# SwiGLU quads in Strassen form: the two 256-column products written as 512-column matmuls, and two of four weight sums moved to GpSimd

## The chip, the cores and the metric

The kernel runs on one core of a Trainium2 chip. The metric is the device time of one execution in microseconds (us); less is better. In the profile PE is the matmul engine (TensorE), PEld its weight load, DVE the VectorE, ACT the ScalarE, POOL the GpSimd and SP the SyncE, which here issues the loads. Tile names in the profile begin with the part of the program that they belong to: a0 and b0 are the first and the second SwiGLU block (FFN) of layer 0, a1 and b1 those of layer 1, m0 and m1 the mixers between a layer's two FFNs. They run in the order a0, m0, b0, a1, m1, b1.

## The reference

```python
SEQ = 512; D_MODEL = 1024; D_FF = 2816; DEPTH = 2

def swiglu(x, w_gu, w_down):
    g, u = jnp.split(x @ w_gu, 2, axis=-1)
    return (jax.nn.silu(g) * u) @ w_down

h = x
for i in range(DEPTH):
    h = h + 0.5 * swiglu(rmsnorm(h, ffn1_norm[i]), ffn1_w_gu[i], ffn1_w_down[i])
    ...   # mixer: convolution, attention, gates, w_o
    h = h + 0.5 * swiglu(rmsnorm(h, ffn2_norm[i]), ffn2_w_gu[i], ffn2_w_down[i])
    ...   # gated input embedding
return rmsnorm(h, final_norm)
```

Everything is fp32. The change touches the four SwiGLUs alone, and in them the product with `w_gu` (1024 x 5632) and the first steps of the product with `w_down`.

## The kernel before

**Numbers.** An fp32 operand is split into a high part h and a low part l of the type fp32r, so that one fp32 product takes three matmuls: h by h, h by l, l by h. For weights the split is ACT's copy `wh` (line 72) and DVE's difference `wl` (line 73), each on a tile of 128 x 1024 that holds eight 128 x 128 weight tiles.

**Strassen.** `w_gu` is computed in quads. A quad takes two features' gate and up columns (a11, a12, a21, a22 are the four quarter blocks of its weights, each one 128 x 1024 tile `st`) and both halves of the 512 rows (256 rows each), and replaces eight quarter products with seven, numbered by j = 1 to 7 (`step`). Class `Quad` forms the weight operands out of the quarters: a11, a12 and a22 as they are, and four sums, all on DVE: a11 - a21 (line 153), a22 - that = s (155), a21 + a22 (158) and a12 - s (150). Class `Halved` forms the operands on the side of the activations, once for each FFN.

**Two ways to issue a product.** A product has h·h, h·l and l·h parts over 4 row blocks and 2 weight tiles each. `joint` (P1, P2, P3, P4, P6) sends h and l of the activations as one operand of 512 columns (`wide`: 8 matmuls with `wh`), and then the high part alone by `wl` (`narrow`: 8 matmuls of 256 columns). The 512 columns land in the two halves of a PSUM tile (`[:, :, :H]` and `[:, :, H:]`), which are added when the tile is read: ACT copies one half, and DVE adds the other (`out`, lines 559 and 560). `product` (P5, P7) sends 24 matmuls of 256 columns, all into one half.

**Chains.** P1 fills tile b. ACT copies b into a new tile a (`seed`, line 555), and P2 adds to a. P6 adds to b, and ACT copies b into d. P5 adds to the right half of d, which ACT then copies out as c5; P7 adds to the left half of b, and DVE adds c5 (line 582), which is one output; P3 adds to d, P4 to b. The PSUM pools PB (tiles b, and whole projections) and PA (tiles a and d) each hold two such tiles.

**Order.** An FFN ends each quad's output with `finish` (a multiply by the row norm on DVE, SiLU on ACT, a multiply on DVE) and with a split of the result into h and l. `next_quad` puts the steps of two successive quads in a row: P1 of the next, P4 of this one, a fill, P2, P6, a fill, P5, P7, P3, two fills. A fill is one accumulation of the down projection: 12 matmuls of 512 columns into a tile `pd`, over four features. The first FFN (a0) does four features without quads and 9 quads; the others do two features and 10 quads each, 39 in all. A scheduler then places every engine's instructions by the dependences and its own costs, so an engine's order can differ from the program's text; each engine executes its own list in order and waits on semaphores of the others. SP loads the raw weights `st` ahead, as far as buffers come free.

Of the kernel before, what the change touches and what calls it, by code (L numbers as in the profile page):

```python
# [130 lines left out]
class Quad:  # L131


    def __init__(self, W, quarters):
        self.W = W
        for q in ("a11", "a21", "a22", "a12"):
            setattr(self, q, W.raw(quarters[q]))

    def part(self, j):

        W = self.W
        tt = W.nc.vector.tensor_tensor
        if j == 1:
            return W.split(self.a11)
        if j == 2:
            return W.split(self.a12)
        if j == 4:
            return W.split(self.a22)
        if j == 3:
            tt(self.a12, self.a12, self.s, ALU.subtract)  # L150
            return W.split(self.a12)
        if j == 6:
            tt(self.a11, self.a11, self.a21, ALU.subtract)  # L153
            self.s = W.buffer("s")
            tt(self.s, self.a22, self.a11, ALU.subtract)  # L155
            return W.split(self.s)
        if j == 5:
            tt(self.a21, self.a21, self.a22, ALU.add)  # L158
            return W.split(self.a21)
        return W.split(self.a11)  # L160

# [22 lines left out]
def trunk_kernel(ctx, tc, dims, x, p, positions, gains, rope_c, final_row, weights, out):  # L184
# [52 lines left out]
    def PB(name):  # L237
        return two(banks.chain, name)
# [211 lines left out]
    class Halved:  # L450


        def __init__(self, nm, l, name):
            self.nm, self.l, self.name = nm, l, name
            self.ys = {p_: [] for p_ in range(1, 8)}
            self.half = {}

# [9 lines left out]
        def own(self, j, xs):  # L467

            H = S // 2
            left, right = slice(0, H), slice(H, S)  # L470
            x, t = G(f"{self.name}x{j}"), G(f"{self.name}t{j}")
            nc.scalar.mul(x, h[j], gain(self.nm, self.l, j))
            nc.vector.tensor_tensor(t[:, left], x[:, right], x[:, left], ALU.subtract)
            th, tl = G(f"{self.name}t{j}h", F32R), G(f"{self.name}t{j}l", F32R)
            self.ys[1].append(self.both(xs[j], left))
            self.ys[5].append((th[:, left], tl[:, left]))
            self.half[j] = x, t, th, tl

        def other(self, j, xs):

            H = S // 2
            left, right = slice(0, H), slice(H, S)
            k = j + KD // 2
            x, t, th, tl = self.half.pop(j)
            y, u = G(f"{self.name}y{j}"), G(f"{self.name}u{j}")
            nc.scalar.mul(y, h[k], gain(self.nm, self.l, k))
            nc.vector.tensor_tensor(t[:, right], y[:, right], x[:, right], ALU.subtract)
            nc.vector.tensor_tensor(u[:, left], t[:, right], x[:, left], ALU.add)
            nc.vector.tensor_tensor(u[:, right], y[:, left], u[:, left], ALU.subtract)
            split_to(th, tl, t)  # L490
            self.ys[7].append((th[:, right], tl[:, right]))
            for p_, at in ((2, left), (3, right)):
                self.ys[p_].append(self.both(xs[k], at))
            for p_, at in ((6, left), (4, right)):
                v = G(f"{self.name}u{j}_{p_}", F32R).rearrange("p (a t) -> p a t", t=H)
                split_to(v[:, 0, :], v[:, 1, :], u[:, at])
                self.ys[p_].append((v[:, 0, :], v))

    class Sevens:
# [7 lines left out]
        def __init__(self, w, l, name, ys, columns, done):  # L507
            self.w, self.l, self.name, self.ys, self.columns, self.done = w, l, name, ys, columns, done
            self.todo = {}
            self.narrow_first = ()  # L510

        def quad(self, n):
            if n not in self.todo:
                cs = self.columns(n)
                quarters = {f"a{a_ + 1}{b_ + 1}": [(self.w, self.l, (4 * b_ + k) * P, c) for k in range(4) for c in cs[a_]]
                            for a_ in range(2) for b_ in range(2)}
                self.todo[n] = {"w": Quad(W, quarters)}
            return self.todo[n]

        def tile(self, n, what):  # L520
# [2 lines left out]
        def joint(self, ps, d, j):  # L523

            hi, lo = d["w"].part(j)
            at = [slice(i * P, (i + 1) * P) for i in range(8)]
            def wide(last):
                for k, (_, pair) in enumerate(self.ys[j]):
                    for w in range(2):
                        nc.tensor.matmul(ps[:, w, :].rearrange("p (a t) -> p a t", t=self.H), hi[:, at[2 * k + w]], pair,  # L530
                                         start=j == 1 and k == 0, stop=last and k == 3, skip_group_check=True)

            def narrow(last):
                for k, (vh, _) in enumerate(self.ys[j]):
                    for w in range(2):
                        nc.tensor.matmul(ps[:, w, :self.H], lo[:, at[2 * k + w]], vh, start=False, stop=last and k == 3,
                                         skip_group_check=True)

            parts = (narrow, wide) if j in self.narrow_first else (wide, narrow)
            for i, part in enumerate(parts):  # L540
                part(i == 1)
# [12 lines left out]
            d[what] = PA(f"{self.name}{n}{what}")  # L554
            nc.scalar.copy(d[what].rearrange("p w t -> p (w t)"), d["b"].rearrange("p w t -> p (w t)"))

        def out(self, n, ps, f, c):
            t = self.tile(n, f"o{f}{c}")
            nc.scalar.copy(t, ps[:, :, self.H:])
            nc.vector.tensor_tensor(t, ps[:, :, :self.H], t, ALU.add)  # L560
            self.done(n, f, c, t, t)

        def step(self, n, j):
# [8 lines left out]
            elif j == 6:  # L572
                self.joint(d["b"], d, j)
                self.seed(n, "d")
            elif j == 5:
                self.product(d["d"][:, :, H:], d, j)
                d["c5"] = self.tile(n, "c5")
# [13 lines left out]
    def ffn(l, nm, name, first=False, beside=iter(()), early=2):  # L591
# [2 lines left out]
        nf = DFF // P  # L594
        W.close()
        acts = {}
        ys = Halved(nm, l, name)
        n_whole = 4 if first else 2
        n0 = n_whole // 2

# [1 line left out]
        def finish(n, f, c, src, t):  # L602
# [9 lines left out]
            if whole:  # L612
# [41 lines left out]
        def fill():  # L654
            if downs:
                m, f0 = downs.pop(0)
                down(m, f0, f0 + 4)

        def next_quad(n):

            for i, j in enumerate((1, 4, None, 2, 6, None, 5, 7, 3, None, None)):
                next(beside, None)
                if j is None:
                    if i < 9 or downs and downs[0][1] < f_last:
                        fill()
                    continue
                step(n if j == 4 else n + 1, j)
                if j == 6 and n % 2:
                    downs.extend((m, 2 * n - 2) for m in range(KD))
# [43 lines left out]
        else:  # L713
# [624 lines left out]
```

## Time and profile before

| what | value |
|---|---|
| median of three runs | 2251.29 us (2251.19 to 2251.89) |
| profiled execution | 2251.37 us, of which the span of instructions is 2249.2 us |
| granted TensorE clock, mean | 0.999 |
| PE busy | 2240.2 us, 100% of the span, 12140 matmuls |
| DVE busy | 1743.6 us, 78% |
| ACT busy | 1455.7 us, 65% |
| POOL busy | 37.3 us, 2%, 42 instructions |
| loads (queue q1) | 220.28 MB, 29.2% of the DMA engines' time |

A row of the timeline has the start in us from the span's start, the duration in us, the engine, the line of the kernel, the operation, output and inputs by name, and in brackets how long the engine was idle before it and what released it. Matmuls are pipelined: the duration of one reaches into the next, and what counts is the distance from start to start.

### The profile page before, as it was taken

The numbers are of one execution on the slowest core, as the hardware profiler recorded it, in microseconds if no ns is written. First come the engines' busy times: TensorE is split into PE (matmuls) and PEld (weight loads), VectorE is DVE, ScalarE is ACT, GpSimd is POOL, SyncE is SP. The second block draws the span as 40 slices with busy tenths as digits, with TensorE's granted clock in tenths as the row PEclk, the third lists the DMA queues.
The fourth block names the chain that finished last, engine by engine and source line by source line (L and its number), as shares of the span: only waits on it lengthen the run. The fifth ranks groups of instructions, "written<-read, shape, count | busy, mean of one in ns | idle before, by whom it ended". The sixth has DMA issues, their size and how long they took to land.

```text
span 2249.2 us, 31135 instructions
## 1 busy us (share of the span) xinstructions
PE 2240.2 (100%) x12140; PEld 1946.9 (87%) x12140; DVE 1743.6 (78%) x2454; ACT 1455.7 (65%) x2246; POOL 37.3 (2%) x42
## 2 busy tenths in 40 slices
PE   9999999999999999999999999999999999999998
PEld 8888888888888888888888888888888888888887
DVE  8987768798866887776797777687889678777756
ACT  7666666576744666667676666664767457666665
POOL 0000000000200000000000000000001000000000
PEclk9999999999999999999999999999999999999999
DMA  5333332323132232334223233323222223333331
GB/s 216 99 113 104 103 123 75 112 75 104 48 104 84 94 103 97 108 105 141 75 94 104 95 106 109 113 87 102 92 77 75 94 75 101 106 103 103 106 101 38
DMA packets 63362, 223.04 MB, mean 99 GB/s; under 512 B 7280, under 2 KB 7280, under 8 KB 63216
## 3 DMA queue, kind: packets, MB, share of 16 engines
q1 hardware_dynamic: 62640, 220.28, 29.2%
q8 instruction: 95, 1.56, 0.3%
q10 hardware_dynamic: 576, 0.79, 0.1%
q14 instruction: 51, 0.42, 0.1%
HBM read 218.94 MB, written 2.10 MB: 98 GB/s over the span
## 4 chain that ended last, share of the span: by engine, by line
PE 96%; DVE 3%; ACT 1%; issue 0%
PE b1pd L269 2%; PE a1pd L269 2%; PE b0pd L269 2%; PE a0pd L269 2%; PE b0pd L271 2%; PE a1pd L271 2%; PE b0pd L270 2%; PE b1pd L271 2%; PE b1pd L270 2%; PE a1pd L270 2%; PE a0pd L270 2%; PE a0pd L271 2%; DVE wl L73 1%; PE e1pg L1134 1%; PE e1pg L1136 1%; PE e1pg L1135 1%
## 5 line engine op out<-in xcount | busy, mean ns | idle before, releaser
L73 DVE TENSOR_TENSOR wl<-st,wh 128x1024 fp32r<-128x1024 f32 (+1 forms) x508 | 614.5, 1212 | 227.2 <-ACT wh L72 223.8
L72 ACT CAST wh<-st 128x1024 fp32r<-128x1024 f32 (+1 forms) x507 | 527.6, 1043 | 305.3 <-PE m1Bp L270 13.9
L72 ACT CAST wh<-s 128x1024 fp32r<-128x1024 f32 x49 | 51.4, 1050 | 29.2 <-PE m1Cp L270 4.2
L73 DVE TENSOR_TENSOR wl<-s,wh 128x1024 fp32r<-128x1024 f32 x49 | 59.6, 1217 | 0.3 <-ACT wh L72 0.3
L153 DVE TENSOR_TENSOR st<-st,st 128x1024 f32<-128x1024 f32 x49 | 59.7, 1218 | 0.2
L155 DVE TENSOR_TENSOR s<-st,st 128x1024 f32<-128x1024 f32 x49 | 59.7, 1218 | 0.1
L150 DVE TENSOR_TENSOR st<-st,s 128x1024 f32<-128x1024 f32 x49 | 59.6, 1216 | 0.0
L158 DVE TENSOR_TENSOR st<-st,st 128x1024 f32<-128x1024 f32 x49 | 59.6, 1216 | 0.0
L647 ACT ACTIVATE h<-a0pd 128x512 f32<-128x512 f32 x40 | 23.7, 592 | 5.6 <-PE a0pd L271 5.4
L647 ACT ACTIVATE h<-b1pd 128x512 f32<-128x512 f32 x40 | 23.6, 590 | 4.9 <-PE b1pd L271 4.8
L647 ACT ACTIVATE h<-b0pd 128x512 f32<-128x512 f32 x40 | 23.6, 590 | 4.8 <-PE b0pd L271 4.7
L647 ACT ACTIVATE h<-a1pd 128x512 f32<-128x512 f32 x40 | 23.5, 589 | 4.5 <-PE a1pd L271 4.4
L643 ACT ACTIVATE b0pd<-h 128x512 f32<-128x512 f32 x40 | 24.0, 599 | 0.6
L643 ACT ACTIVATE b1pd<-h 128x512 f32<-128x512 f32 x40 | 24.0, 599 | 0.6
L643 ACT ACTIVATE a1pd<-h 128x512 f32<-128x512 f32 x40 | 23.9, 598 | 0.7
L643 ACT ACTIVATE a0pd<-h 128x512 f32<-128x512 f32 x40 | 23.9, 599 | 0.6
L108 POOL MEMSET wh<- 128x256 f32 x4 | 1.1, 313 | 1172.8 <-DVE wl L73 1172.8
L269 PE MATMUL a0p<-a0x,wh 128*128 128x512 f32 x44 | 17.1, 390 | 0.0
L270 PE MATMUL a0p<-a0x,wh 128*128 128x512 f32 x44 | 17.1, 390 | 0.0
L271 PE MATMUL a0p<-a0x,wl 128*128 128x512 f32 x44 | 17.1, 389 | 0.0
L264 ACT ACTIVATE b1x<-h,cols 128x512 fp32r<-128x512 f32 x8 | 5.8, 724 | 13.3 <-DVE h L1063 13.3
L264 ACT ACTIVATE b0x<-h,cols 128x512 fp32r<-128x512 f32 x8 | 5.8, 724 | 13.3 <-DVE h L1063 13.3
(6949 smaller groups left out, 7502.7 us busy)
## 6 DMA issues: line engine op xcount, KB each, us to landing
st<-in_weights SPq DMA_DIRECT2D x406, 512.0 KB, 3.3
st<-in_weights SPq DMA_DIRECT2D x8, 256.0 KB, 5.2
h<-in_x SPq DMA_DIRECT2D x7, 256.0 KB, 5.3
out<-e1d SPq DMA_DIRECT2D x4, 256.0 KB, 2.1
out<-fh SPq DMA_DIRECT2D x3, 256.0 KB, 2.0
e0pi<-in_p SPq DMA_DIRECT2D x2, 256.0 KB, 4.0
e1pi<-in_p SPq DMA_DIRECT2D x2, 256.0 KB, 3.7
fg<-in_final_row SPq DMA_DIRECT2D x2, 256.0 KB, 5.0
```

What stands on the lines that cost most here:

```text
L72: self.nc.scalar.copy(hi[:, w], src[:, w])
L73: self.nc.vector.tensor_tensor(lo[:, w], src[:, w], hi[:, w].bitcast(F32), ALU.subtract)
L150: tt(self.a12, self.a12, self.s, ALU.subtract)
L153: tt(self.a11, self.a11, self.a21, ALU.subtract)
L155: tt(self.s, self.a22, self.a11, ALU.subtract)
L158: tt(self.a21, self.a21, self.a22, ALU.add)
L269: nc.tensor.matmul(ps, wh, vh, start=first, stop=False, skip_group_check=seeded)
L270: nc.tensor.matmul(ps, wh, vl, start=False, stop=False, skip_group_check=seeded)
L271: return nc.tensor.matmul(ps, wl, vh, start=False, stop=last, skip_group_check=seeded)
L643: nc.scalar.mul(ps, h[m], 2.0)
L647: nc.scalar.mul(h[m], ps, 0.5)
L1134: nc.tensor.matmul(o, vh[:, toks(t)], wh, start=first, stop=False)
```

## The change

- P5 and P7 of the FFNs become `joint` products with a 512-column operand (`fresh = (1, 7)`, `merged=True`; `Halved.other` now lays th and tl out as that operand, by two splits of 256 columns in place of one of 512). P7 gets a PSUM tile e of its own from PB and starts it afresh. c5 and P7's value are each formed by a copy and an add (`sum`), DVE adds P7's value to b, and POOL adds it to c5, which is then the output.
- Of the four weight sums a11 - a21 and a21 + a22 go to POOL, asked for at j = 1. The first goes to a buffer d of its own, and s is written over a11.
- One of the two fills at the end of `next_quad` moves between P5 and P7.
- In the FFNs other than the first, the down projections m = 0 and 1 are begun with feature 0 alone after the first quad's P3; the later fill then does the features left.

```diff
 class Quad:
@@ part
         if j == 1:
+            if self.by_pool:
+                self.d = W.buffer("d")
+                W.nc.gpsimd.tensor_tensor(self.d, self.a11, self.a21, ALU.subtract)
+                W.nc.gpsimd.tensor_tensor(self.a21, self.a21, self.a22, ALU.add)
             return W.split(self.a11)
...
         if j == 6:
-            tt(self.a11, self.a11, self.a21, ALU.subtract)
-            self.s = W.buffer("s")
+            if self.by_pool:
+                self.s, self.a11 = self.a11, self.d
+            else:
+                tt(self.a11, self.a11, self.a21, ALU.subtract)
+                self.s = W.buffer("s")
             tt(self.s, self.a22, self.a11, ALU.subtract)
             return W.split(self.s)
         if j == 5:
-            tt(self.a21, self.a21, self.a22, ALU.add)
+            if not self.by_pool:
+                tt(self.a21, self.a21, self.a22, ALU.add)
             return W.split(self.a21)
@@ Halved.other
-            split_to(th, tl, t)
-            self.ys[7].append((th[:, right], tl[:, right]))
+            if self.merged:
+                for p_, at, v in ((5, left, th), (7, right, tl)):
+                    v = v.rearrange("p (a t) -> p a t", t=H)
+                    split_to(v[:, 0, :], v[:, 1, :], t[:, at])
+                    self.ys[p_].append((v[:, 0, :], v))
+            else:
+                split_to(th, tl, t)
+                self.ys[7].append((th[:, right], tl[:, right]))
@@ Sevens
-                                         start=j == 1 and k == 0, stop=last and k == 3, skip_group_check=True)
+                                         start=j in self.fresh and k == 0, stop=last and k == 3, skip_group_check=True)
...
-        def out(self, n, ps, f, c):
-            t = self.tile(n, f"o{f}{c}")
+        def sum(self, n, what, ps):
+            t = self.tile(n, what)
             nc.scalar.copy(t, ps[:, :, self.H:])
             nc.vector.tensor_tensor(t, ps[:, :, :self.H], t, ALU.add)
+            return t
+
+        def out(self, n, ps, f, c):
+            t = self.sum(n, f"o{f}{c}", ps)
             self.done(n, f, c, t, t)
@@ Sevens.step
+            elif j == 5 and 7 in self.fresh:
+                self.joint(d["d"], d, j)
+                d["c5"] = self.sum(n, "c5", d["d"])
+            elif j == 7 and 7 in self.fresh:
+                e = PB(f"{self.name}{n}e")
+                self.joint(e, d, j)
+                p = self.sum(n, "p7", e)
+                nc.vector.tensor_tensor(d["b"][:, :, H:], d["b"][:, :, H:], p, ALU.add)
+                t = d.pop("c5")
+                nc.gpsimd.tensor_tensor(t, t, p, ALU.add)
+                self.done(n, 1, 1, t, t)
@@ ffn
+        sevens.fresh = (1, 7)
...
                 m, f0 = downs.pop(0)
-                down(m, f0, f0 + 4)
+                begun = pds.pop(m, None)
+                down(m, f0 + (begun is not None), f0 + 4, begun, first_=begun is None)
...
-            for i, j in enumerate((1, 4, None, 2, 6, None, 5, 7, 3, None, None)):
+            for i, j in enumerate((1, 4, None, 2, 6, None, 5, None, 7, 3, None)):
...
             step(n0, 7)
             step(n0, 3)
+            for m in range(2):
+                pds[m] = down(m, 0, 1, last=False)
```

How the rows move is shown at three places; "waits" lists the engines and queues whose semaphores a row waits for, and a number behind a name is a buffer's.

First the matmuls of quad 6 of the first FFN on PE. Before, from the last three matmuls of P5 (operand t0 to t3, into d) to the first three of P7 (into b):

```order
L550 MATMUL a06d<-a0t3h,wh_1825 128x256
L550 MATMUL a06d<-a0t3l,wh_1825 128x256
L550 MATMUL a06d<-a0t3h,wl_1826 128x256
L550 MATMUL a06b<-a0t0h,wh_1855 128x256
L550 MATMUL a06b<-a0t0l,wh_1855 128x256
L550 MATMUL a06b<-a0t0h,wl_1856 128x256
```

After the change, from the last matmuls of the fill that now stands between P5 and P7, over all of P7 (into e), to the start of P3:

```order
L278 MATMUL a0pd_1_1816<-a0a11l,wh_1776 128x512
L279 MATMUL a0pd_1_1816<-a0a11h,wl_1777 128x512
L545 MATMUL a06e<-a0t0l,wh_1832 128x512 x2
L545 MATMUL a06e<-a0t1l,wh_1832 128x512 x2
L545 MATMUL a06e<-a0t2l,wh_1832 128x512 x2
L545 MATMUL a06e<-a0t3l,wh_1832 128x512 x2
L551 MATMUL a06e<-a0t0l,wl_1833 128x256 x2
L551 MATMUL a06e<-a0t1l,wl_1833 128x256 x2
L551 MATMUL a06e<-a0t2l,wl_1833 128x256 x2
L551 MATMUL a06e<-a0t3l,wl_1833 128x256 x2
L551 MATMUL a06d<-a0x_161,wl_1863 128x256 x2
```

P5 is written like P7 now, and stands before the fill. The rows of 256 columns with the high and the low part of an operand have become rows of 512 columns (x2: for the two weight tiles), the tile e is new, and b is no longer touched here.

Next DVE, and POOL beside it, in the same quad. Before, DVE from the add of P7's value (line 582) over two multiplies of `finish` (606) to the third and the fourth weight split and the first weight sum (153) of quad 7:

```order
L582 TENSOR_TENSOR a06c_1853<-a06b,a06c_1853 128x512 [waits PE_49,Activation_49]
L606 TENSOR_TENSOR a06c_1853<-a06c_1853,a0r 128x512 [waits DVE_49]
L73 TENSOR_TENSOR wl_1965<-st_1955,wh_1964 128x1024 [waits DMAHW5_49,Activation_49]
L611 TENSOR_TENSOR a0an_1886<-a06c_1853 128x256 [waits Activation_49]
L153 TENSOR_TENSOR st_1955<-st_1955,st_1957 128x1024 [waits DMAHW6_49,DVE_49]
L560 TENSOR_TENSOR a06o_1909<-a06d,a06o_1909 128x512 [waits Activation_49]
L73 TENSOR_TENSOR wl_1987<-st_1679,wh_1986 128x1024 [waits Activation_49]
L606 TENSOR_TENSOR a06o_1909<-a06o_1909,a0r 128x512 [waits DVE_49]
L73 TENSOR_TENSOR wl_2032<-st_1961,wh_2031 128x1024 [waits DMAHW0_49,PE_49,Activation_49]
```

After, from c5's sum (line 575) on; 162 is the sum s, 154 the sum a12 - s, 601 the add of P7's value to b, 636 the multiply of `finish`:

```order
L575 TENSOR_TENSOR a06c_1813<-a06d,a06c_1813 128x512 [waits Activation_49]
L73 TENSOR_TENSOR wl_1926<-st_1913,wh_1925 128x1024 [waits DMAHW5_49,PE_49,Activation_49]
L162 TENSOR_TENSOR st_1913<-st_1917,d 128x1024 [waits DMAHW7_49,DVE_49,Pool_49]
L73 TENSOR_TENSOR wl_1948<-st_1647,wh_1947 128x1024 [waits PE_49,Activation_49]
L575 TENSOR_TENSOR a06p_1852<-a06e,a06p_1852 128x512 [waits Activation_49]
L601 TENSOR_TENSOR a06b<-a06b,a06p_1852 128x2x256 [waits DVE_49]
L636 TENSOR_TENSOR a06c_1813<-a06c_1813,a0r 128x512 [waits Pool_49]
L73 TENSOR_TENSOR wl_1993<-st_1919,wh_1992 128x1024 [waits DMAHW0_49,Activation_49]
L641 TENSOR_TENSOR a0an_1859<-a06c_1813 128x256 [waits Activation_49]
L154 TENSOR_TENSOR st_1919<-st_1919,st_1913 128x1024 [waits DVE_49]
```

And POOL's whole list from quad 5's last instruction to quad 8's weight sums (the st of the first pair, 1913 to 1917, are quad 7's):

```order
L603 TENSOR_TENSOR a05c_1543<-a05c_1543,a05p_1582 128x512 [waits DVE_49]
L146 TENSOR_TENSOR d<-st_1913,st_1915 128x1024 [waits DMAHW5_49,DMAHW6_49,DMAHW3_49,DVE_49]
L147 TENSOR_TENSOR st_1915<-st_1915,st_1917 128x1024 [waits DMAHW7_49,Pool_49]
L603 TENSOR_TENSOR a06c_1813<-a06c_1813,a06p_1852 128x512 [waits DVE_49]
L146 TENSOR_TENSOR d<-st_2183,st_2185 128x1024 [waits DMAHW3_49,DMAHW4_49,DMAHW1_49,DVE_49]
L147 TENSOR_TENSOR st_2185<-st_2185,st_2187 128x1024 [waits DMAHW5_49,Pool_49]
```

POOL's two sums of quad 7 (lines 146 and 147) have left DVE, which waits for the first of them at line 162; c5 goes through POOL (603), for which DVE waits at the multiply 636, and the weight split that followed that multiply's counterpart still stands behind it.

Last ACT at the first quad of b0, whose output c5 is ready before b02a is seeded. Before (578 is the copy of c5, 643 begins a down projection, 607 is SiLU, 559 a copy of `out`, 555 the seed):

```order
L578 COPY b01c_7206<-b01d 128x512 [waits PE_49,Activation_49]
L634 ACTIVATE b0gn_7208<-b0gn_7208 128x512 [waits DVE_49]
L72 CAST wh_7343<-st_7288 128x1024 [waits DMAHW3_49,PE_49]
L643 ACTIVATE b0pd_0_7395<-h_89 128x512
L261 CAST b0a1h<-b0un_7209 128x512 [waits DVE_49]
L607 ACTIVATE b01c_7206<-b01c_7206 128x256 [waits DVE_49]
L643 ACTIVATE b0pd_1_7511<-h_90 128x512
L72 CAST wh_7373<-s 128x1024 [waits PE_49]
L559 COPY b01o_7272<-b01d 128x512
L72 CAST wh_7399<-st_7397 128x1024 [waits DMAHW4_49,PE_49,Activation_49]
L555 COPY b02a<-b02b 128x1024 [waits DVE_49,PE_49]
L607 ACTIVATE b01o_7272<-b01o_7272 128x256 [waits DVE_49]
```

After (574 is the copy in `sum`, 665 and 637 SiLU, 674 begins a down projection, 570 is the seed):

```order
L574 COPY b01c_7124<-b01d 128x512 [waits PE_49,Activation_49]
L665 ACTIVATE b0gn_7127<-b0gn_7127 128x512 [waits DVE_49]
L674 ACTIVATE b0pd_0_7198<-h_89 128x512
L72 CAST wh_7248<-st_6962 128x1024 [waits DMAHW4_49,PE_49]
L674 ACTIVATE b0pd_1_7209<-h_90 128x512 [waits DVE_49]
L269 CAST b0a1h<-b0un_7128 128x512 [waits DVE_49]
L574 COPY b01p_7158<-b01e 128x512 [waits PE_49]
L72 CAST wh_7278<-st_7220 128x1024 [waits DMAHW4_49,PE_49]
L637 ACTIVATE b01c_7124<-b01c_7124 128x256 [waits DVE_49]
L72 CAST wh_7306<-st_7214 128x1024 [waits PE_49,Activation_49]
L574 COPY b01o_7188<-b01d 128x512
L570 COPY b02a<-b02b 128x1024 [waits DVE_49,PE_49]
```

The seed of b02a stands behind the SiLU of c5 in both, but c5 now comes after P7's copy, DVE's two adds and POOL's add, and both down projections are begun ahead of P7's copy.

More of the change, by code (lines that the diff above doesn't have):

```diff
@@ L131, with __init__ @@
 class Quad:
-    def __init__(self, W, quarters):
-        self.W = W
+    def __init__(self, W, quarters, by_pool=False):
+        self.W, self.by_pool = W, by_pool
         for q in ("a11", "a21", "a22", "a12"):
@@ L450, in trunk_kernel, with __init__ @@
     class Halved:
-        def __init__(self, nm, l, name):
-            self.nm, self.l, self.name = nm, l, name
+        def __init__(self, nm, l, name, merged=False):
+            self.nm, self.l, self.name, self.merged = nm, l, name, merged
             self.ys = {p_: [] for p_ in range(1, 8)}
@@ L475, in own @@
             self.ys[1].append(self.both(xs[j], left))
-            self.ys[5].append((th[:, left], tl[:, left]))
+            if not self.merged:
+                self.ys[5].append((th[:, left], tl[:, left]))
             self.half[j] = x, t, th, tl
@@ L509, in __init__ @@
             self.todo = {}
-            self.narrow_first = ()
+            self.narrow_first, self.fresh = (), (1,)
         def quad(self, n):
@@ L516, in quad @@
                             for a_ in range(2) for b_ in range(2)}
-                self.todo[n] = {"w": Quad(W, quarters)}
+                self.todo[n] = {"w": Quad(W, quarters, 7 in self.fresh)}
             return self.todo[n]
@@ L596, in ffn @@
         acts = {}
-        ys = Halved(nm, l, name)
+        ys = Halved(nm, l, name, True)
         n_whole = 4 if first else 2
@@ L656, in fill @@
                 m, f0 = downs.pop(0)
-                down(m, f0, f0 + 4)
+                begun = pds.pop(m, None)
+                down(m, f0 + (begun is not None), f0 + 4, begun, first_=begun is None)
         def next_quad(n):
-            for i, j in enumerate((1, 4, None, 2, 6, None, 5, 7, 3, None, None)):
+            for i, j in enumerate((1, 4, None, 2, 6, None, 5, None, 7, 3, None)):
                 next(beside, None)
                 if j is None:
-                    if i < 9 or downs and downs[0][1] < f_last:
+                    if i in (2, 5) or downs and downs[0][1] < f_last:
                         fill()
```

## The prediction

> **What bounds the kernel now.** I read the page first (its busy shares and the chain that ended last), then PE's waits, then PE's timeline over one quad, then the other engines' over the same stretch.
>
> ```profile
> span 2249.2 us, 31135 instructions
> ...
> PE 2240.2 (100%) x12140; PEld 1946.9 (87%) x12140; DVE 1743.6 (78%) x2454; ACT 1455.7 (65%) x2246; POOL 37.3 (2%) x42
> ...
> PE 96%; DVE 3%; ACT 1%; issue 0%
> ```
>
> ```profile
> PE idle L379 <- DVE hpi L306: 1.0, 1, 1.0
> PE m1cop L271 <- DVE wl L73: 0.3, 1, 0.3
> PE m0cop L271 <- DVE wl L73: 0.3, 1, 0.3
> PE a0pd L269 <- ACT a0a2h L261: 0.2, 1, 0.2
> ```
>
> PE is the bound: busy all through, 96% of the chain, and its waits come to 1.8 us. No wait is left to remove. The time falls only by what PE spends less, and rises by every wait that is new. The profiled execution took 2251.37 us (2.2 outside the span), 0.08 above the median of 2251.29; I forecast from 2251.4.
>
> **What PE spends.** PE's timeline of quad 6, and the first quad of b0, where no 512-column matmul comes before P1:
>
> ```profile
> 178.08 1.12 PE L536 MATMUL a06b<-a0u,wl 128*128 128x256 f32 x8
> 179.04 2.00 PE L530 MATMUL a06b<-a0u,wh 128*128 128x512 f32 x8
> 180.88 0.39 PE L269 MATMUL a0pd<-a0a8h,wh 128*128 128x512 f32 x1
> 181.11 0.39 PE L270 MATMUL a0pd<-a0a8l,wh 128*128 128x512 f32 x1
> ...
> 183.60 0.28 PE L550 MATMUL a06d<-a0t0h,wh 128*128 128x256 f32 x1
> 183.72 0.28 PE L550 MATMUL a06d<-a0t0l,wh 128*128 128x256 f32 x1
> ...
> 186.48 0.28 PE L550 MATMUL a06b<-a0t0h,wh 128*128 128x256 f32 x1
> ...
> 189.36 1.12 PE L536 MATMUL a06d<-a0x,wl 128*128 128x256 f32 x8
> ```
>
> ```profile
> 764.96 1.12 PE L536 MATMUL b01d<-b0x,wl 128*128 128x256 f32 x8
> 765.91 2.00 PE L530 MATMUL b01d<-b0x,wh 128*128 128x512 f32 x8
> 767.75 1.98 PE L530 MATMUL b02b<-b0x,wh 128*128 128x512 f32 x8
> 769.57 1.11 PE L536 MATMUL b02b<-b0x,wl 128*128 128x256 f32 x8
> 770.52 1.12 PE L536 MATMUL b01b<-b0u,wl 128*128 128x256 f32 x8
> ...
> 773.32 1.98 PE L530 MATMUL b02a<-b0x,wh 128*128 128x512 f32 x8
> ```
>
> P5 runs from 183.60 to 186.48 and P7 to 189.36, 2.88 us each, 0.12 for each of 24 matmuls. A joint product with the wide part first (P1: 767.75 to 770.52) takes 2.77: eight of 512 columns at 0.227 and eight of 256 at 0.12. The columns are the same; what goes is the fixed part of eight matmuls. So P5 and P7 save 2 x (2.88 - 2.77) = 0.22. Where 512 columns follow 256 there is a small loss: the wide part takes 765.91 to 767.75 = 1.84 behind a narrow one and 1.82 first. The fill that now follows P5's narrow part adds one such switch, about 0.03. Net 0.19 a quad. The clock was 0.999 throughout, so no gain or loss is put there. **39 quads x 0.19 = 7.4 us.**
>
> **DVE and POOL in a steady quad.**
>
> ```profile
> 180.00:210.50 30.50, 30.50 (x177) 27.04 (x176) 22.99 (x28) 19.97 (x29) 0.00 (x0) 1.00 0.32 107
> 110.00:120.00 10.00, 10.00 (x60) 8.90 (x60) 10.00 (x14) 6.53 (x10) 0.00 (x0) 1.00 0.28 91
> ```
>
> ```profile
> 183.38 1.23 DVE L73 TENSOR_TENSOR wl<-st,wh 128x1024 fp32r<-128x1024 f32 x1 [0.51 <-ACT wh L72]
> 187.63 1.23 DVE L73 TENSOR_TENSOR wl<-st,wh 128x1024 fp32r<-128x1024 f32 x1 [3.03 <-ACT wh L72]
> 189.62 0.69 DVE L582 TENSOR_TENSOR a06c<-a06b,a06c 128x512 f32<-128x512 f32 x1 [0.77 <-PE a06b L550]
> ...
> 192.43 1.21 DVE L153 TENSOR_TENSOR st<-st,st 128x1024 f32<-128x1024 f32 x1
> ...
> 220.19 0.69 DVE L582 TENSOR_TENSOR a07c<-a07b,a07c 128x512 f32<-128x512 f32 x1 [0.77 <-PE a07b L550]
> ```
>
> In one period (line 582 comes again after 30.57) DVE is busy 22.99 of 30.50 (fourth column of the first row; ACT 19.97). The change takes away two sums of 1.21 and line 582 (0.69), and adds three operations of 512 columns (c5's sum, P7's sum, the add to b): 3 x 0.69 - 2 x 1.21 - 0.69 = -1.0. ACT gets one copy more of some 0.6. The two 256-column splits in place of one in `Halved` are four times an FFN, under 0.3 us, beside PE. The change loads the same weights; SP waits for other DVE splits to free buffers, but PE's waits show none on a load. The moved fill costs PE nothing more, nor do the one-feature downs, whose matmuls the later fill lacks.
>
> What POOL costs, the trace of before shows only for other instructions, with one input from SBUF:
>
> ```profile
> 586.49 0.60 POOL L984 TENSOR_SCALAR m0s11e<-m0s11e,m0s11sm 128x128 f32<-128x128 f32 x1 [1.65 <-DVE m0s11sm L983]
> ...
> 587.82 1.20 DVE L73 TENSOR_TENSOR wl<-st,wh 128x1024 fp32r<-128x1024 f32 x1
> ...
> 587.99 3.26 POOL L984 TENSOR_SCALAR m0s11e<-m0s11e,m0s11sm 128x384 f32<-128x384 f32 x1 [0.90 <-DVE m0s11sm L983]
> ...
> 589.02 1.20 DVE L73 TENSOR_TENSOR wl<-st,wh 128x1024 fp32r<-128x1024 f32 x1
> ```
> ```profile
> L984 POOL TENSOR_SCALAR m0s20e<-m0s20e,m0s20sm 128x384 f32<-128x384 f32 x1 | 1.2, 1247 | 2.0 <-DVE m0s20sm L983 2.0
> ```
>
> From 128 to 384 columns POOL goes from 0.60 to 1.25, 2.5 ns a column; carried on, 1024 columns are 2.85 us and 512 are 1.57 (estimates from these rows). 2 x 2.85 + 1.57 = 7.3 a quad of 30.4: POOL keeps up. But beside two DVE subtractions the 384 columns took 3.26, 2.0 more, while those subtractions took their usual 1.20. So the two engines do get in each other's way, here at POOL's expense. A DVE subtraction that begins during a POOL operation isn't in this trace; it may be delayed by nothing or by the whole POOL operation.
>
> [...]
>
> I take no loss for PE in a steady quad. POOL's sums begin after the split ahead of line 162 in order, in the stretch that leads up to 187.63, where DVE idles most (the 3.03). The price of a full block there is 5.7 us, of which idle time of 3.03, 0.77 and 0.51 takes 4.3; the remaining 1.4 comes off the lead of the splits ahead of PE. The split of 183.38 is done at 184.61 and wanted by P3 at 189.36 (above): 4.75, so more than that. DVE's multiply 636 waits for POOL's line 603, 1.57 after P7's sum; the add 601 (0.69) lies beside it, so DVE stands about 0.9 a quad, which the -1.0 pays. Queued behind it are a weight split and c5's SiLU.
>
> ```profile
> 135.08 1.21 DVE L73 TENSOR_TENSOR wl<-st,wh 128x1024 fp32r<-128x1024 f32 x1
> ```
> ```profile
> 139.23 1.12 PE L536 MATMUL a04b<-a0u,wl 128*128 128x256 f32 x8
> ```
>
> This is the split with the shortest lead that I found between 60 and 150 us: ready at 136.29, used at 139.23, so 2.94 ahead. It follows a stretch in the first FFN in which DVE, with the rotary tables besides, is busy 10.00 of 10.00 (the second window above). There POOL is held off by back-to-back subtractions, line 162 comes late, and nothing idle absorbs it. Two or three quads of up to 2.85 + 0.9 each, less 1.0, add up to 5 to 8 against a lead of 2.94. Bounds: a gain of 0.2 (the wait before a0pd above may go, two sums being gone from DVE) and a loss of 5. I take a loss of 0.7, nearer the low end, since DVE only waits here for what POOL still lacks.
>
> **The starts of b0, a1, b1.** There no fill covers the first quad's end.
>
> ```profile
> 770.24 0.68 DVE L560 TENSOR_TENSOR b01o<-b01d,b01o 128x512 f32<-128x512 f32 x1
> ```
> ```profile
> 766.64 0.60 ACT L261 CAST b0a1h<-b0un 128x512 fp32r<-128x512 f32 x1
> ...
> 771.01 1.00 ACT L555 COPY b02a<-b02b 128x1024 f32<-128x1024 f32 x1
> ```
>
> Before, b01d is read out by DVE at 770.24, its PSUM is free at 770.92, the seed of b02a is done at 772.01, and P2 wants it at 773.32: 1.3 to spare. After: P3 ends at 767.75 - 0.2 = 767.5. P7's copy (0.6) follows the cast that ended at 767.24, and its sum (0.7) is done by about 768.5, so e is free before the two one-feature downs (2 x 3 x 0.227 = 1.36) end at 768.9; this wait costs nothing, with 0.4 to spare. P1 and P4 end at 774.5, and another feature (0.68), which the order has ahead of P2, at 775.2. But the seed now follows P7's sum, POOL's 1.57, the multiply 636 (0.69), a split, an L641 and a sum (1.2, 0.4, 1.2) and then b01o's sum: 768.5 + 1.6 + 0.7 + 2.8 + 0.7 = 774.3, the seed's 1.0 makes 775.3, and a delay of 0.5 by POOL 775.8. P2 waits 0.1 to 0.6, and the seed of d comes as late after it. Bounds: nothing, or 1.1 if both come late. I take 0.5, **3 x 0.5 = 1.5 us.** In the first FFN fills cover its start.
>
> **The sum:** 2251.4 - 7.4 + 0.7 + 1.5 = 2246.2 us, 0.23% less. About 0.2%, 4.5 us, is what a measurement here can tell from no change; the bound for faster is 2246.8.
>
> **Rivals.**
> - *Nothing new waits.* 2251.4 - 7.4 = 2244.0, and 2243.6 with the small wait of a0pd gone. For it: 22 of 30.4 us of DVE, and the lead of 4.75. Against: the chain above. Chance 0.2.
> - *The saving is spent in the starts and in the saturated stretch.* 3 x 1.1 and 5: 2251.4 - 7.4 + 8.3 = 2252.3 at most; half of it 2248.2. Chance 0.2.
> - [...] If DVE is blocked for every POOL operation and the 1.4 of above comes on top of a late line 162 (2.85) and the 0.9 of line 636, 5.2 in one quad passes the lead of 4.75. It decides at 7.4 / 39 = 0.19 us a quad; 0.5 a quad gives 2251.4 - 7.4 + 19.5 = 2263.5. Against it: 1.2 to 1.4 us of DVE are free behind even that in each period, so no backlog builds. [...] Chance 0.11.
> - *The 512-column rows gain nothing*, if P5 and P7 keep 2.88: 2251.4 + 2.2 = 2253.6 with my waits, 2251.4 without. Every joint product on the page speaks against it. Chance 0.03.
>
> My forecast has the rest, 0.46; its own range is 2244.8 to 2248, some two thirds below 2246.8. Faster: 0.2 + 0.31 = 0.51. Same (2246.8 to 2255.8): 0.15 + 0.19 + 0.02 = 0.36. Slower 0.13. The range from 2243.5 to 2252.3 leaves out most of the third rival and a little of the others.
>
> **What would show it.** PE's instructions fall by 39 x 16 = 624; the period of L575 on a c5 tile from quad to quad is 30.38 where L582's was 30.57. PE's waits list b02a, a12a, b12a on ACT's seed with 0.1 to 1.1 each, and a0-tiles with 0.7 in all. POOL's 1024-column rows last 2.2 to 3.3 us in idle stretches of DVE and more beside subtractions. DVE shows idle time before line 636 put down to POOL. I am wrong if PE lists waits for `wl` in the quads, if the 1024-column rows on POOL take over 5 us, or if DVE's subtractions beside POOL last or wait clearly more than 1.2 us.

## The result and the profile after

The change made the kernel slower: 2328.43 us (median of 4 runs, 2327.11 to 2330.82) against 2251.24, a ratio of 1.0344 with an interval of 1.0331 to 1.0356. I had forecast 2246.2 and a range up to 2252.3; the third rival came true in its cause, that POOL's operations block DVE, at four times its price and by another path.

One correction first. The description of the kernel before says that pool PA holds two tiles; it holds one. The tiles a and d of a quad take turns in it, so that the seed of d waits until DVE has read a out. Much hangs on this.

The page of after, the parts that answer to those of before (span, busy time, chain):

```profile
span 2325.3 us, 30316 instructions
...
PE 2252.2 (97%) x11516; PEld 1913.4 (82%) x11516; DVE 1864.2 (80%) x2470; ACT 1475.7 (63%) x2301; POOL 329.1 (14%) x159
...
PE 71%; DVE 14%; issue 8%; ACT 5%; POOL 2%; DMA 1%; ACTq 0%; POOLq 0%; DVEq 0%
```

PE has 624 matmuls fewer, as the diff says, but is no longer the whole chain. Its waits, from the longest (columns: what waits, for what, us in total, times, longest):

```profile
PE a0pd L277 <- ACT a0a7h L269: 4.5, 1, 4.5
PE a0pd L277 <- ACT a0a2h L269: 3.3, 1, 3.3
PE a13d L545 <- ACT a13d L570: 2.7, 1, 2.7
...
PE a06d L545 <- ACT a06d L570: 1.6, 1, 1.6
PE a08d L545 <- ACT a08d L570: 1.6, 1, 1.6
```

P5 of every quad in the steady row waits 1.6 us for the seed of its tile d (line 570). Quad 6 again, the same stretch as before, on DVE, on ACT (the seed) and on POOL:

```profile
192.34 1.22 DVE L73 TENSOR_TENSOR wl<-st,wh 128x1024 fp32r<-128x1024 f32 x1
193.47 0.42 DVE L641 TENSOR_TENSOR a0an<-a05o 128x256 f32<-128x256 f32 x1
194.02 3.22 DVE L73 TENSOR_TENSOR wl<-st,wh 128x1024 fp32r<-128x1024 f32 x1
197.17 2.88 DVE L270 TENSOR_TENSOR a0a11l<-a0an,a0a11h 128x512 fp32r<-128x512 f32 x1
199.97 1.21 DVE L73 TENSOR_TENSOR wl<-d,wh 128x1024 fp32r<-128x1024 f32 x1
201.11 0.68 DVE L575 TENSOR_TENSOR a06o<-a06a,a06o 128x512 f32<-128x512 f32 x1
```
```profile
201.87 1.00 ACT L570 COPY a06d<-a06b 128x1024 f32<-128x1024 f32 x1 [4.94 <-DVE a06o L575]
```
```profile
193.64 2.52 POOL L146 TENSOR_TENSOR d<-st,st 128x1024 f32<-128x1024 f32 x1 [10.60 <-DVE wl L73]
196.24 3.26 POOL L147 TENSOR_TENSOR st<-st,st 128x1024 f32<-128x1024 f32 x1
```

POOL's first sum ends at 196.16, and the split that DVE began at 194.02 ends at 197.24, 1.08 later: it did its work only when POOL was done, and lasted 3.22 in place of 1.23. The second sum ends at 199.50, and the 0.68 us of line 270 that began at 197.17 end at 200.05. POOL was held in its turn: 196.16 - 193.89 (end of line 641) and 199.50 - 197.24 are both 2.27 us, close to the 2.40 us of such a sum's shortest row. So here each holds the other out for a whole instruction. DVE loses 2.0 + 2.2 = 4.2 us, the sum that reads tile a (line 575) ends at 201.79, the seed at 202.87, and P5, due at 201.2, starts at 202.92. (A row at a0's start, shown at the end, does not fit this. These 2.27 to 2.40 us are less than the 2.85 that I had worked out for such a sum from the rows of another operation; no row of before gave the 2.2 that I named as its shortest time.)

Before, the same stretch had this margin:

```profile
179.98 0.68 DVE L560 TENSOR_TENSOR a06o<-a06a,a06o 128x512 f32<-128x512 f32 x1
```
```profile
181.08 1.00 ACT L555 COPY a06d<-a06b 128x1024 f32<-128x1024 f32 x1 [1.79 <-PE a06b L530]
```

The seed waited for P6 alone, was done at 182.08, and P5 came at 183.60: 1.5 to spare, and another 0.4 for DVE's sum. A delay of 4.2 goes through 1.9 of margin and the 0.64 that DVE idled before its last split, and 1.7 remains, in each quad.

**Where the 77 us are.** The distance from P1 to P1 of successive quads, from PE's timelines (us; "first three" is the sum of an FFN's first three distances, a0 and b0 shown; a1 and b1 are as b0, within 2.8):

| kernel | steady quad | first three, a0 | first three, b0 | time |
|---|---|---|---|---|
| before | 30.57 | 98.0 | 86.4 | 2251.2 |
| the change | 32.25 | 112.6 | 92.9 | 2328.4 |
| sums on DVE | 30.37 | 99.3 | 88.2 | 2253.9 |
| POOL sums alone, old products | 32.40 | 113.5 | 92.1 | 2328.5 |
| memsets on POOL | 30.37 | 99.2 | 87.1 | 2249.7 |
| sums held back | 30.37 | 105.8 | 90.9 | 2272.4 |
| sums in quarters | 30.37 | 107.6 | 90.4 | 2270.6 |
| one block | 30.37 | 102.9 | 88.2 | 2257.7 |
| first two quads old | 30.37 | 99.2 | 86.1 | 2247.0 |

There are 23 steady distances: 23 x 1.68 = 39 us. The twelve first ones add 14.6 + 6.5 + 9.3 + 6.5 = 37.

### The profile page after: what moved, and what is told of

Same layout as the page of the kernel before. It is cut to its first block, busy times and chain, and to the rows that moved or that the text cites. A ratio compares the mean times of both kernels' runs of the same rounds, so it can differ in the third digit from the quotient of the medians.

```text
span 2325.3 us, 30316 instructions
## 1 busy us (share of the span) xinstructions
PE 2252.2 (97%) x11516; PEld 1913.4 (82%) x11516; DVE 1864.2 (80%) x2470; ACT 1475.7 (63%) x2301; POOL 329.1 (14%) x159
## 4 chain that ended last, share of the span: by engine, by line
PE 71%; DVE 14%; issue 8%; ACT 5%; POOL 2%; DMA 1%; ACTq 0%; POOLq 0%; DVEq 0%
DVE wl L73 5%; ACT wh L72 2%; PE b1pd L278 1%; PE b1pd L277 1%; PE b1pd L279 1%; PE a0pd L277 1%; PE b0pd L277 1%; PE b0pd L278 1%; PE a0pd L278 1%; PE a0pd L279 1%; PE b0pd L279 1%; PE a1pd L277 1%; PE a1pd L278 1%; PE a1pd L279 1%; POOL d L146 1%
## 5 line engine op out<-in xcount | busy, mean ns | idle before, releaser
L73 DVE TENSOR_TENSOR wl<-st,wh 128x1024 fp32r<-128x1024 f32 (+1 forms) x508 | 673.7, 1328 | 187.4 <-ACT wh L72 174.2
L146 POOL TENSOR_TENSOR d<-st,st 128x1024 f32<-128x1024 f32 x39 | 108.4, 2778 | 664.4 <-DVE wl L73 637.1
L147 POOL TENSOR_TENSOR st<-st,st 128x1024 f32<-128x1024 f32 x39 | 122.8, 3149 | 3.1
L73 DVE TENSOR_TENSOR wl<-d,wh 128x1024 fp32r<-128x1024 f32 x39 | 50.0, 1281 | 2.5 <-ACT wh L72 2.5
L162 DVE TENSOR_TENSOR st<-st,d 128x1024 f32<-128x1024 f32 x39 | 47.7, 1224 | 2.6
L154 DVE TENSOR_TENSOR st<-st,st 128x1024 f32<-128x1024 f32 x39 | 47.5, 1219 | 0.0
L72 ACT CAST wh<-d 128x1024 fp32r<-128x1024 f32 x39 | 40.6, 1040 | 3.5 <-PE b02a L545 0.9
L72 ACT CAST wh<-s 128x1024 fp32r<-128x1024 f32 x10 | 10.5, 1052 | 12.9 <-PE m1Cp L278 4.2
```

Source lines behind the costliest of these rows:

```text
L72: self.nc.scalar.copy(hi[:, w], src[:, w])
L73: self.nc.vector.tensor_tensor(lo[:, w], src[:, w], hi[:, w].bitcast(F32), ALU.subtract)
L146: W.nc.gpsimd.tensor_tensor(self.d, self.a11, self.a21, ALU.subtract)
L147: W.nc.gpsimd.tensor_tensor(self.a21, self.a21, self.a22, ALU.add)
```

## The experiments

**All sums on DVE.**

```diff
-                self.todo[n] = {"w": Quad(W, quarters, 7 in self.fresh)}
+                self.todo[n] = {"w": Quad(W, quarters)}
```

> The change with all four weight sums of a quad on DVE again; P5 and P7 as 512-column products, the tile e, the add of c5 on POOL and the one-feature starts stay. Theory 1 (POOL's two weight sums hold up DVE's operations with two SBUF inputs, so that DVE reads tile a late, the seed of d is late and P5 waits 1.73 us): the wait of P5 on the seed is gone, the quads come every 30.4 us, and the time is 2244 to 2250 us. Theory 2 (the new chain with e, c5 and three more DVE operations is what is late, wherever the sums are formed): P5 still waits 1 us or more, DVE has 2.4 us more to do, and the time is above 2310 us.

2253.94 us, ratio to before 1.0011 (1.0002 to 1.0021). No steady quad waits, and the distance is 30.37, where 30.38 was forecast. So theory 2 falls, and the matmuls gain what was worked out. Yet the time is 4 to 10 us above theory 1's: the starts of b0, a1 and b1 lose 1.9 each, a0's 1.3, 7.0 in sum, more than the 23 x 0.20 = 4.6 that the steady quads gain.

```profile
PE b02d L545 <- ACT b02d L570: 1.5, 1, 1.5
PE a12d L545 <- ACT a12d L570: 1.5, 1, 1.5
PE b12d L545 <- ACT b12d L570: 1.5, 1, 1.5
PE a0pd L277 <- ACT a0pd L674: 1.3, 1, 1.3
```

**The sums on POOL, nothing else.** The kernel before with the `by_pool` branches of `Quad` for the FFNs' quads.

> The kernel before with only the two weight sums of each FFN quad moved to POOL; P5 and P7 as they were. Theory 1: d's buffer comes free at the same split of a fill, so POOL starts at the same place, DVE is held for about 4 us there, and P5 waits for the seed of d by 1 to 2 us in each steady quad: 2290 to 2330 us, with P5's wait on the page. Theory 2: no such wait; DVE has 2.4 us less to do, 2249 to 2255 us.

2328.54 us, 1.0342 (1.0325 to 1.0359), as theory 1 said: P5 waits 1.6 us, the distance is 32.40, and the two sums alone cost as much as the whole change. DVE's rows are those of the change:

```profile
194.89 3.22 DVE L73 TENSOR_TENSOR wl<-st,wh 128x1024 fp32r<-128x1024 f32 x1
198.03 2.88 DVE L270 TENSOR_TENSOR a0a11l<-a0an,a0a11h 128x512 fp32r<-128x512 f32 x1
```

**The add of c5 on DVE.**

```diff
-                nc.gpsimd.tensor_tensor(t, t, p, ALU.add)
+                nc.vector.tensor_tensor(t, t, p, ALU.add)
```

> The change with the add of P7's value to c5 (line 603) on DVE in place of POOL; the two weight sums stay on POOL. Theory 1: the sums still hold DVE, P5 still waits 1.7 us, 2322 to 2332 us. Theory 3 (DVE's wait for POOL's add, 0.7 us in each quad at the multiply 636, pushes the rest late): P5's wait shrinks by 0.5 us or more, below 2310 us.

2342.06 us in one run, slower than both theories said; P5 still waits 1.6, the distance settles at 32.24 again, and the starts and one or two quads behind them grow (b0's first three to 95.8). Theory 3 falls: DVE's wait for this one POOL add isn't what holds P5. About half of the 13.6 us more can be read from the granted clock: it was 0.50 for seven stretches of 3.41 us, 23.9 us in all against 10.2 in the change (0.994 in the mean against 0.997), which is 6.8 us of work. Why the starts wait longer I did not follow up.

**Memsets on POOL.**

```diff
+N_SET = 2
...
-                W.nc.gpsimd.tensor_tensor(self.d, self.a11, self.a21, ALU.subtract)
-                W.nc.gpsimd.tensor_tensor(self.a21, self.a21, self.a22, ALU.add)
+                for q in (self.d, self.a21):
+                    for _ in range(N_SET):
+                        W.nc.gpsimd.memset(q, 0.0)
```

> The change with POOL's two weight sums replaced by four memsets of 128 x 1024 on the same two buffers (so the weight sums are left out: P5, P6, P7 and P3 get other weights). POOL then only writes to SBUF, for about as long (4 x 1.1 us, from the 313 ns of a 256-column memset). Theory 1, with the block on the read side: DVE's subtractions keep 1.2 us, P5 waits for nothing, 2244 to 2252 us. Theory 1 with a block by any access of POOL to SBUF: the same stretched rows of 3 us on DVE and P5's wait of 1.5 us or more, 2315 to 2330 us.

2249.74 us in one run, the distance 30.37, as the theory of a block on the read side said. The kernel leaves both sums out. POOL wrote in the same stretch and DVE's split beside it took its usual time:

```profile
207.93 1.97 POOL L149 MEMSET d<- 128x1024 f32 x2 [10.57 <-DVE wl L74]
```
```profile
208.28 1.23 DVE L74 TENSOR_TENSOR wl<-st,wh 128x1024 fp32r<-128x1024 f32 x1
209.42 0.69 DVE L272 TENSOR_TENSOR a0a13l<-a0an,a0a13h 128x512 fp32r<-128x512 f32 x1
```

So it isn't POOL's being busy, nor its writes to SBUF; what is left is POOL's reading, an inference that no run tests alone. The other pair of memsets (193.10 to 195.07) ran earlier, beside line 164 and a split, which took their usual 1.23 and 1.22. A memset was shorter than a sum (0.95 us, not 2.4), so this shows the absence of a hold and is not a test at equal length.

**The sums held back.** POOL reads one column of quad n's first output, and the sums of quad n+1 queue behind it.

```diff
+            if f == c == 0:
+                mark = nc.gpsimd.tensor_tensor(tick, acts[i][:, 0:1], acts[i][:, 0:1], ALU.add)
+                sevens.later = lambda: tc.issue_after(mark.ins)
...
+                with self.later():
                     W.nc.gpsimd.tensor_tensor(self.d, self.a11, self.a21, ALU.subtract)
                     W.nc.gpsimd.tensor_tensor(self.a21, self.a21, self.a22, ALU.add)
```

> The change with POOL's two weight sums of quad n+1 held back until DVE has finished the first output of quad n (one 128 x 1 add on POOL reads that output, and the sums are queued behind it); the same sums on POOL, about 10 us later. Theory 1 (POOL holds DVE wherever it runs, but what cost the time is that it did so ahead of the sum that frees tile a for the seed of d): DVE's rows are still stretched to 2 to 3 us beside POOL, but P5's wait in the steady quads falls under 0.3 us and the period to 30.4; with the starts somewhat late, 2250 to 2262 us. Rival (the DVE time that POOL takes, 4 us a quad, is too much in any place): the period stays at 31.5 us or more, the time above 2295 us.

2272.38 us, 1.0094 (1.008 to 1.0107); above theory 1's range, far below the rival's. In the steady quad DVE is held for just as long, two splits taking 6.54 in place of 2.4:

```profile
193.26 2.40 POOL L147 TENSOR_TENSOR d<-st,st 128x1024 f32<-128x1024 f32 x1
195.74 3.26 POOL L148 TENSOR_TENSOR st<-st,st 128x1024 f32<-128x1024 f32 x1
```
```profile
190.46 0.68 DVE L578 TENSOR_TENSOR a06o<-a06a,a06o 128x512 f32<-128x512 f32 x1
...
193.54 6.54 DVE L73 TENSOR_TENSOR wl<-st,wh 128x1024 fp32r<-128x1024 f32 x2 [0.52 <-ACT wh L72]
```

But tile a's sum (here line 578) is already past, the hold falls where DVE idled 2.85 us with all sums on DVE, and the distance is 30.37. The same hold costs 1.7 us or nothing, by where it falls. At the starts, where DVE has no such place, the first three distances of the four FFNs grow by 23.5 us in sum.

**One sum on POOL**, the other on DVE.

```diff
-                W.nc.gpsimd.tensor_tensor(self.a21, self.a21, self.a22, ALU.add)
...
-            if not self.by_pool:
-                tt(self.a21, self.a21, self.a22, ALU.add)
+            tt(self.a21, self.a21, self.a22, ALU.add)
```

> The change with only a11 - a21 on POOL; a21 + a22 is on DVE again. Theory 1: one block of some 2 us in place of two; of the 4.2 us that DVE's sum of tile a came late, 1.73 showed on PE, so with 2 us less the wait of P5 in the steady quad is gone, period 30.4, and the time 2252 to 2262 us. Rival (it isn't the length of the block but that POOL is used there at all, since line 162 and the sums wait for it): P5 still waits 1 us or more, above 2290 us.

2303.88 us in one run; P5 still waits 1.5, as the rival had it. The rows tell why, and not for the rival's reason:

```profile
183.86 3.27 DVE L73 TENSOR_TENSOR wl<-st,wh 128x1024 fp32r<-128x1024 f32 x1
187.06 0.68 DVE L268 TENSOR_TENSOR a0a11l<-a0an,a0a11h 128x512 fp32r<-128x512 f32 x1
187.66 1.21 DVE L164 TENSOR_TENSOR st<-st,st 128x1024 f32<-128x1024 f32 x1
188.80 1.22 DVE L73 TENSOR_TENSOR wl<-d,wh 128x1024 fp32r<-128x1024 f32 x1
189.93 0.68 DVE L573 TENSOR_TENSOR a06o<-a06a,a06o 128x512 f32<-128x512 f32 x1
```
```profile
191.37 0.42 ACT L635 ACTIVATE a06o<-a06o 128x256 f32<-128x256 f32 x1 [1.75 <-DVE a06o L634]
191.70 1.01 ACT L568 COPY a06d<-a06b 128x1024 f32<-128x1024 f32 x1
```

Line 270's counterpart is no longer held, but the scheduler put the other sum (164) into the same gap, and on ACT the SiLU of that output ahead of the seed, 1.1 later than DVE freed the tile. The experiment changed two things more than the one it meant to. Leaving the second sum out altogether keeps both orders:

> The change with POOL's second sum (a21 + a22) left out altogether, so P5 has other weights; a11 - a21 stays on POOL. Unlike the version that formed the second sum on DVE, DVE's and ACT's orders around the seed of d are those of the change, so that only the number of blocks differs. Theory 1 (each POOL sum holds DVE once for about 2 us; the second of them is what makes the seed late): tile a's sum comes 2.2 us earlier than in the change, the seed of d is done 0.5 us before P5 wants it, period 30.37, and the time 2250 to 2260 us. Rival (any POOL sum in this place costs the wait): period 31.5 or more, above 2285 us.

2257.66 us in one run, distance 30.37, no wait of a steady P5, as theory 1 said:

```profile
181.53 3.28 DVE L73 TENSOR_TENSOR wl<-st,wh 128x1024 fp32r<-128x1024 f32 x1
184.74 0.68 DVE L269 TENSOR_TENSOR a0a11l<-a0an,a0a11h 128x512 fp32r<-128x512 f32 x1
...
186.48 0.68 DVE L574 TENSOR_TENSOR a06o<-a06a,a06o 128x512 f32<-128x512 f32 x1
```
```profile
187.24 1.00 ACT L569 COPY a06d<-a06b 128x1024 f32<-128x1024 f32 x1 [2.79 <-DVE a06o L574]
```

One hold of 2.0 fits into the margin; the second is what the steady quads paid for.

**Each sum in four pieces.**

```diff
-                W.nc.gpsimd.tensor_tensor(self.d, self.a11, self.a21, ALU.subtract)
-                W.nc.gpsimd.tensor_tensor(self.a21, self.a21, self.a22, ALU.add)
+                for out, x, y, op in ((self.d, self.a11, self.a21, ALU.subtract), (self.a21, self.a21, self.a22, ALU.add)):
+                    for w in (slice(c, c + 256) for c in range(0, 1024, 256)):
+                        W.nc.gpsimd.tensor_tensor(out[:, w], x[:, w], y[:, w], op)
```

> The change with each of POOL's two weight sums written as four of 256 columns. Theory 1 with a lock for each whole instruction: DVE gets in behind a POOL instruction of some 0.7 us, so that its subtraction is held once for at most 0.7 us and not 2.0, and POOL is then held by DVE; P5's wait falls from 1.73 to under 0.6 us, and the time below 2285 us. [...]

2270.62 us in one run, distance 30.37, no steady wait. DVE's splits beside POOL take 1.57 and 1.76:

```profile
186.67 5.37 POOL L148 TENSOR_TENSOR d<-st,st 128x256 f32<-128x256 f32 x4 [10.60 <-DVE wl L73]
192.01 4.53 POOL L148 TENSOR_TENSOR st<-st,st 128x256 f32<-128x256 f32 x4
```
```profile
187.04 1.57 DVE L73 TENSOR_TENSOR wl<-st,wh 128x1024 fp32r<-128x1024 f32 x1
188.53 1.23 DVE L271 TENSOR_TENSOR a0a11l<-a0an,a0a11h 128x512 fp32r<-128x512 f32 x1
189.68 1.76 DVE L73 TENSOR_TENSOR wl<-d,wh 128x1024 fp32r<-128x1024 f32 x1
```

The sums take 9.9 us now and not 5.8: POOL is the one that waits (for a piece alone my estimate is 0.75, from 1.30 for the 512 columns of c5's add and 2.40 for 1024; eight are 6.0). DVE is held for no more than one instruction of POOL, by 0.3 and 0.5 us in these two splits where a whole sum held a split by 2.0, so here the length of a hold was set by how the sum is written. The time was 14 us below the bound that theory 1 gave.

**Which quads of the start lose.** The first two quads of each FFN with the old products in the old order (n0 is the first), in a second version the first quad alone (n0 + 1 in place of n0 + 2); all sums on DVE, no one-feature starts:

```diff
+        sevens.fresh, sevens.since, sevens.paired = (1, 7), n0 + 2, True
...
-            elif j == 5 and 7 in self.fresh:
+            elif j == 5 and 7 in self.fresh and n >= self.since:
```

> The first two quads of each FFN as in the kernel before (P5 and P7 as 24 matmuls of 256 columns each, old place of the fill, no one-feature starts); from the third quad on the new products with e, and all weight sums on DVE. Theory: a quad in the steady row saves 0.20 us without any wait, and what the version with the sums on DVE lost lies only in the first two quads, where DVE has no spare time. 31 quads x 0.20 = 6.2: 2245 us, between 2244 and 2247, with periods of 30.37 and no wait of P5 on a seed over 0.5 us. Rival (three more DVE operations a quad cost PE something also later, or the change-over from old to new quads costs 1 us in each FFN): 2249 us or more.

> All sums on DVE, and the new products from the second quad of each FFN on (35 quads), with no one-feature starts. Theory (DVE has no spare time in the first two quads, whichever is new): 35 x 0.20 = 7.0 saved, and about 1 us lost in each FFN by a late seed or split in the second quad: 2247 to 2250 us, slower than with the third. Rival (only the first quad, with its normalisation and whole-feature work, is too tight): 2244.5 to 2246.5 us, better than with the third.

2246.97 us, 0.998 (0.9971 to 0.9989), at the upper edge of its theory's range, and 2247.16, 0.9981 (0.9972 to 0.999). The second time lies at the lower edge of its theory's range, but the distances speak for its rival: b0's first three are 85.95, less than the 86.1 of the first version, so the second quad loses nothing. What the version with all sums on DVE lost in b0, a1 and b1 lies in the first quad alone: 88.2 - 85.95 = 2.3 in each, which is the 2253.9 - 2247.2 = 6.8 us. What a0 loses stays in both versions (99.2 and 99.4 against 98.0), although the first has the old products there. Without the one-feature starts that version stays where it was:

```diff
-            for m in range(2):
-                pds[m] = down(m, 0, 1, last=False)
```

> The change with all sums on DVE and without the two down projections begun with one feature. Theory (they cover the time until P7's sum frees e for the next b): P1 of the second quad in b0, a1 and b1 waits 0.5 to 1.5 us more on DVE, the fills later are longer by as much as the early matmuls took, and the time is 2255 to 2259 us against 2253.9. Rival (they only move 1.36 us of matmuls, and the seeds bind anyway): 2252 to 2254.5 us.

2253.41 us, 1.0009 (0.9999 to 1.0018). P1 of the second quad then waits for e as forecast, 0.9 to 1.0 us, but the seeds that waited before no longer do; the rival holds, and this part of the change moves a wait from one place to another.

```profile
PE a12b L545 <- DVE a11p L575: 1.0, 1, 1.0
PE b12b L545 <- DVE b11p L575: 1.0, 1, 1.0
PE b02b L545 <- DVE b01p L575: 0.9, 1, 0.9
```

**The first FFN as before, too:**

```diff
+        ys = Halved(nm, l, name, not first)
+        sevens.fresh, sevens.since, sevens.paired = ((1,), 99, False) if first else ((1, 7), n0 + 2, True)
```

> As the version with the first two quads of each FFN old, but the whole first FFN as in the kernel before (also its activation splits). In that version the first FFN gave nothing: b0 began at 740.75 against 739.92 although seven quads save 0.20 each, so some 2.2 us are lost at its start, where the 256-column splits and another order come in. Theory: with the old first FFN b0 begins at 739.9 again, and the three others each save 8 x 0.20 = 1.6: 2251.1 - 4.9 = 2246.2, between 2245.5 and 2247. Rival (the loss at the first FFN's start is not from the change): b0 begins late by 0.8 again, 2247 to 2248.5.

2246.40 us, 0.9977 (0.9969 to 0.9986): the fastest measured, by 5 us against before, but not clear of the 2246.97 above. Of its theory one half holds: a0's first three distances are 98.2 again, so their loss came with the new layout of the first FFN's operands or its order. But b0 began at 740.85 and not at 739.9, as the rival had it, and 0.8 of that is lost ahead of a0's first quad. P1 of a0's first quad begins 0.3 to 1.9 us later than in the profile of before (38.44) in all of these runs, this one too; what that is stays open.

## Why the prediction was wrong

- **What bounds the kernel, and what PE spends:** right. 0.19 a quad was forecast, 0.20 came, with the 512-column rows at their pitch (P5 took 2.77 us and P7 2.76 with all sums on DVE, against 2.88 before), in every version without a hold.
- **"I take no loss for PE in a steady quad": the step that failed.** Its full-block bound of 5.7 us was above the 4.2 that came; what failed is that idle time and the splits' lead were to absorb it. Three things about it were wrong. First, the place: POOL's sums were put in the stretch up to the idle 3.03. They begin as soon as buffer d, the next of the ring of raw weights, is freed by the fill's split (the row of 192.34, released in POOL's bracket), and that is ahead of DVE's densest stretch; the idle time that was to absorb them comes after. Second, the work that waits: I compared the delay with the lead of weight splits (4.75), and not with the seed of d, whose tile DVE frees on that same list with 1.9 to spare. Third, the one row that I had, in which POOL lost, left open whether DVE would lose too; I said so, and still gave the block only a rival's chance. In the steady quads P5 waited 1.6 us, 23 times, and the distance was 32.25 where I forecast 30.38.
- **The third rival** had the cause, DVE blocked by POOL's operations, and the point from which it decides (0.19 us a quad), but put the lost time down to weight splits, priced it at 0.5 a quad where 1.88 came (32.25 - 30.37), and was given 0.11. Its counterargument, that DVE has free time in each period, was true and beside the point: the order in the period decided here, not its sum.
- **The saturated stretch**, at 0.7 with a bound of 5, cost 14.6 us over the three first distances of a0; the holds on a DVE without idle time passed that bound. That POOL would be held off by back-to-back DVE work in the first FFN was right: two of its sums took 5.5 and 7.4 us, over the 5 that I had named as a sign of being wrong. That DVE only waits there for what POOL still lacks was not: the sums held DVE in their turn. One part of the loss is below, under the clock.
- **The starts of b0, a1, b1:** b02a's wait was put at 0.1 to 0.6 and was 0.4 with the sums on DVE. It was the first of several: the seed of d followed with 1.5, which I had capped at 1.1 for both. With POOL's holds a start costs 6.5 to 9.3.

## What to carry to other kernels

Before work is moved to another engine, look for rows in which the two engines hold each other up (here a POOL sum stretched a DVE split from 1.23 to 3.22 us), and ask for each instruction that it can hold up which tile comes free behind it; the margin is that of the next reader of that tile, not of the engine's mean load. A start that is set by a buffer of a ring comes when the ring says so: find which instruction frees it, and look at what stands next there. And an experiment that moves one instruction also lets the scheduler move others; leaving the instruction out altogether told more than putting it back.

## What the runs showed of the hardware that I had not expected

After the longest of the new waits the matmuls ran at half pace. PE's timeline of after behind the wait of 4.5 us, and windows of it (busy time of PE and the granted clock):

```profile
134.84 0.80 PE L277 MATMUL a0pd<-a0a7h,wh 128*128 128x512 f32 x1 [4.46 <-ACT a0a7h L269]
...
136.82 0.63 PE L278 MATMUL a0pd<-a0a4l,wh 128*128 128x512 f32 x1
137.25 0.63 PE L279 MATMUL a0pd<-a0a4h,wl 128*128 128x512 f32 x1
```
```profile
120.00:130.00 10.00, 9.34 (x49) 1.00 0.31 105
135.00:140.00 5.00, 5.00 (x12) 0.50 0.26 84
```

The matmuls come every 0.427 us in place of 0.227 at a granted clock of 0.50, for about 6 us, so a wait of 4.5 cost some 7.5. In this trace the waits of 1.6 and 2.7 us have no such rows behind them; the one of 3.3 has. But the length of the wait doesn't decide alone: with the add of c5 on DVE a wait of 1.85 (before b07d) was followed by 3.41 us at 0.50, and with one sum on POOL a wait of 3.17 (before a05d) by none. What decides the runs here do not settle.

POOL was also held for longer than one instruction. One of its sums at a0's start, and two rows of DVE:

```profile
52.65 7.35 POOL L146 TENSOR_TENSOR d<-st,st 128x1024 f32<-128x1024 f32 x1 [24.54 <-DVE wl L73]
```
```profile
56.97 0.76 DVE L270 TENSOR_TENSOR a0u<-a0u,a0u 128x256 fp32r<-128x256 f32 x2
57.64 0.69 DVE L664 TENSOR_TENSOR a0gn<-a0pg,a0r 128x512 f32<-128x512 f32 x1
```

From 52.82 to 57.73 DVE began and ended twelve instructions with two SBUF inputs, one behind the other, all after POOL's and all at their usual times. POOL's row ends at 60.00, 2.36 after line 664 began, which has one input in PSUM and was not held. So in this row POOL got in only where DVE did not read two tiles of SBUF. In the steady quads it got in between two such DVE instructions; why there and not here stays open.
